# Top-k of the last prompt tile carried in the sample's rounds; probability scales on ScalarE; weight remainders on GpSimd; an order per layer

## Chip, cores and metric

One core of one Trainium2 chip. The metric is the device time of one execution in microseconds. Five engines work side by side: PE (TensorE), DVE (VectorE), ACT (ScalarE), POOL (GpSimd) and SP (SyncE), whose queue issues all data transfers of this kernel.

## What is computed

One inference step of a two-layer encoder trunk on 512 prompt tokens and 64 sample tokens (the sample has 1024 cached keys). Each layer projects the normalised input to the operands of three mixers, merges their gated outputs and projects back:

```python
z = rmsnorm(x, norm_g) @ w_in                     # aq ak av ag | bq bk bv bqi bki bwi bg | cq ck cv cg | mg
# A: differential attention, 4 heads: p = softmax(q k + bias); a = p[0] - lam * p[1]; o = a v
# B: an indexer scores every key; the top k keys of each query stay, the others are masked
score = jnp.einsum('bqh,bqhs->bqs', wi, relu(qi ki)); _, idx = lax.top_k(score, topk)
p = softmax(q k[idx] * 64 ** -0.5 + bias); o = p v[idx]      # topk: 128 for the prompt, 256 for the sample
# C: retention with a decay per head, in chunks
y = x + sum(sigmoid(mg) * (stack([oa * silu(ag), ob * silu(bg), oc * silu(cg)]) @ w_branch)) @ w_out
```

The outputs are y of the prompt and of the sample, the new keys and values, and the states.

## The kernel before

**Tiles.** The 576 tokens are five tiles: four of 128 prompt tokens (t = 0 to 3) and the 64 of the sample (t = 4). A matrix product with a weight is made exact enough from three products of a rounded high part and a remainder: high x high, (input remainder) x high, high x (weight remainder). `wload` fetches 512 x 256 weights into `wraw`, ACT writes the high part `whi` (L495), and DVE the remainder `wlo = wraw - whi` (L496, 128x1024). `wlo` has two buffers and `wraw` two; a projection of 1024 rows takes a pair of each. `proj_ch` (L634) keeps channels on the partitions (288 columns a product), `proj_tok` (L613 to L622) tokens (256 columns). Both issue the `whi` products of an output tile first and the `wlo` products last. PSUM has three tiles for projections (`pj`), two for scores (`s`) and three for transposes and small outputs (`t`).

**Mixer B's top-k.** `idx_prompt` and `idx_sample` leave scores in SBUF: `SC[t]` for t = 1, 2, 3 (128 partitions, 256, 384 and 512 columns) and `SC[4]` for the sample (64 partitions, 1088 columns; the other 64 partitions of that tile are idle). `topk(t)` finds eight maxima a round (`MAX8`, L829) and strikes them out (`MATCH_REPLACE8`, L830): 16 rounds for a prompt tile, 32 for the sample, and then turns the struck places into 0 and the rest into a large positive number (L831), which `b_prompt` and `b_sample` take as a mask. All of it is on DVE.

**Attention.** For a tile, PE writes scores, DVE adds the bias and finds the minimum (L468, L920, L471), ACT writes the exponential with its sum, DVE takes the reciprocal and multiplies the probabilities by it (L1004 in `a_att`, L1188 in `b_prompt`, L1218 in `b_sample`), and PE transposes them. The bias windows come from a table in DRAM, `grep` (12 heads x 128 rows x 352), which `build_windows` fills by one transfer.

**Norms.** `qknorm` squares on ACT, sums on DVE, takes the power on POOL (L455), multiplies on DVE (L648), multiplies by the gain on POOL (L649); PE's transposes (L946) wait for that.

**The order.** The program is a list of steps (`STEPS`): x: norm of a tile; pw, i, iq: the indexer's weights, projection and queries; w: the bias table; cv, cq, ca: mixer C; aq, ak, av, aa: mixer A; bq, bp, bs: mixer B; g: a gate; s: the split of a gated output; m: the merge of a branch (`branch`, the large products L634); top: the top-k. The steps stand in the same order in both layers, each with a bias for layer 0 and one for layer 1. `Order` records every instruction, gives it its place in the program plus its step's bias as its rank, and plays the program through with a cost for each instruction: each engine takes, of the instructions that are ready, the one of lowest rank. The order of issue so found is pinned on every engine, SP included; an engine's queue runs in that order only.

## Time and profile before

| | |
|---|---|
| median of 3 runs | 1444.93 us (1444.91 to 1447.29) |
| the profiled execution | 1446.73 us, of which the span from first to last instruction 1444.9 |
| PE busy | 1385.6 us, 96% of the span, 10422 products |
| weight loads (PEld) | 1328.2 us, 92% |
| DVE, ACT, POOL busy | 1146.3 (79%), 663.8 (46%), 246.9 us (17%) |
| granted clock of PE, mean | 0.999 |
| DMA engines, mean share; moved | 31.6%; 127.51 MB |

The busy time of PE is that of its records, which overlap: a product's record is longer than the distance to the next product's start. So an engine that waits shortly between two products can still read as busy.

### The profile page before, as it was taken

The numbers are of one execution on the slowest core, as the hardware profiler recorded it, in microseconds if no ns is written. First come the engines' busy times: TensorE is split into PE (matmuls) and PEld (weight loads), VectorE is DVE, ScalarE is ACT, GpSimd is POOL, SyncE is SP. The second block draws the span as 40 slices with busy tenths as digits, with TensorE's granted clock in tenths as the row PEclk, the third lists the DMA queues.
The fourth block names the chain that finished last, engine by engine and source line by source line (L and its number), as shares of the span: only waits on it lengthen the run. The fifth ranks groups of instructions, "written<-read, shape, count | busy, mean of one in ns | idle before, by whom it ended". The sixth has DMA issues, their size and how long they took to land.

```text
span 1444.9 us, 27676 instructions
## 1 busy us (share of the span) xinstructions
PE 1385.6 (96%) x10422; PEld 1328.2 (92%) x10422; DVE 1146.3 (79%) x2791; ACT 663.8 (46%) x1631; POOL 246.9 (17%) x294
## 2 busy tenths in 40 slices
PE   5999999999999999999999999999999999999999
PEld 4899989998999989999989998899989998999999
DVE  5799999998776888844487999999997678886433
ACT  5433464445555464433353335543546454644321
POOL 1121432112223020000030333410321120300000
PEclk9999999999999999999999999999999999999999
DMA  7423225222332222324532222232424322121333
GB/s 220 111 73 86 54 72 141 73 76 86 95 94 61 87 59 59 89 67 115 172 103 64 70 74 77 79 100 70 112 65 114 78 68 61 47 73 47 99 122 115
DMA packets 189738, 127.51 MB, mean 88 GB/s; under 512 B 65976, under 2 KB 188388, under 8 KB 189604
## 3 DMA queue, kind: packets, MB, share of 16 engines
q1 hardware_dynamic: 189604, 125.74, 31.1%
q8 instruction: 82, 1.34, 0.4%
q14 instruction: 52, 0.43, 0.1%
HBM read 114.84 MB, written 13.03 MB: 88 GB/s over the span
## 4 chain that ended last, share of the span: by engine, by line
PE 64%; DVE 20%; ACT 6%; DMA 5%; issue 3%; SPq 1%; POOL 1%; DVEq 0%; ACTq 0%
PE pj L634 29%; PE pj L622 11%; PE pj L1352 6%; DVE wlo L496 4%; DVE u L830 3%; DMA wraw<-in_w_in_dram 3%; DVE m L829 3%; PE s L1181 1%; PE t L1193 1%; ACT whi L495 1%; DVE s L468 1%; PE s L998 1%; DVE u L956 1%; PE t L1013 1%; PE t L1045 1%
## 5 line engine op out<-in xcount | busy, mean ns | idle before, releaser
L495 ACT CAST whi<-wraw 128x1024 fp32r<-128x1024 f32 x164 | 172.0, 1049 | 186.6 <-DMA wraw<-in_w_in_dram 73.3
L496 DVE TENSOR_TENSOR wlo<-wraw,whi 128x1024 fp32r<-128x1024 f32 x164 | 199.3, 1226 | 64.7 <-PE pj L634 53.0
L634 PE MATMUL pj<-xh,whi 128*128 128x288 f32 x1216 | 205.9, 299 | 5.3 <-ACT sg L1265 1.9
L634 PE MATMUL pj<-xh,wlo 128*128 128x288 f32 x1216 | 199.8, 297 | 3.9 <-DVE wlo L496 3.9
L634 PE MATMUL pj<-xl,whi 128*128 128x288 f32 x1216 | 200.4, 297 | 0.0
L634 PEld LDWEIGHTS pj<-xh,whi 128*128 128x128 f32 x1216 | 175.0, 188 | 9.1 <-ACT sg L1265 2.3
L634 PEld LDWEIGHTS pj<-xh,wlo 128*128 128x128 f32 x1216 | 173.4, 188 | 7.0 <-DVE wlo L496 5.6
L634 PEld LDWEIGHTS pj<-xl,whi 128*128 128x128 f32 x1216 | 174.1, 188 | 1.2 <-issue 0.3
L829 DVE MAX8 m<-u 64x8 f32<-64x1088 f32 (+3 forms) x160 | 134.9, 845 | 1.7
L830 DVE MATCH_REPLACE8 u<-m,u 64x1088 f32<-64x1088 f32 (+3 forms) x160 | 133.1, 832 | 0.1
L622 PE MATMUL pj<-wlo,xh 128*128 128x256 f32 x768 | 121.5, 289 | 6.5 <-DVE wlo L496 6.4
L455 POOL TENSOR_TENSOR ssn<-ssn,mh 128x4 f32<-128x4 f32 (+1 forms) x70 | 73.2, 1048 | 318.6 <-DVE ssn L454 313.1
L634 PE MATMUL pj<-u,whi 128*128 128x288 f32 x768 | 126.1, 297 | 0.0
L622 PE MATMUL pj<-whi,xh 128*128 128x256 f32 x768 | 117.8, 287 | 3.6 <-ACT whi L495 2.4
L622 PE MATMUL pj<-whi,xl 128*128 128x256 f32 x768 | 115.2, 285 | 0.0
L622 PEld LDWEIGHTS pj<-wlo,xh 128*128 128x128 f32 x768 | 103.1, 191 | 10.0 <-DVE wlo L496 8.5
L634 PEld LDWEIGHTS pj<-u,whi 128*128 128x128 f32 x768 | 110.1, 188 | 0.7
L622 PEld LDWEIGHTS pj<-whi,xh 128*128 128x128 f32 x768 | 102.2, 190 | 6.5 <-ACT whi L495 3.7
L622 PEld LDWEIGHTS pj<-whi,xl 128*128 128x128 f32 x768 | 101.7, 191 | 0.4
L1265 ACT ACTIVATE sg<-pj 128x288 f32<-128x288 f32 x96 | 39.2, 410 | 77.9 <-PE pj L634 77.1
L634 PE MATMUL pj<-u,wlo 128*128 128x288 f32 x384 | 70.5, 299 | 1.2 <-DVE wlo L496 1.2
L1352 PE MATMUL pj<-whi,u 128*128 128x256 f32 x512 | 68.8, 282 | 0.4 <-ACT u L1287 0.4
(280 smaller groups left out, 2547.1 us busy)
## 6 DMA issues: line engine op xcount, KB each, us to landing
wraw<-in_w_in_dram SPq DMA_DIRECT2D x116, 512.0 KB, 3.8
wraw<-in_w_branch_dram SPq DMA_DIRECT2D x24, 512.0 KB, 4.7
wraw<-in_w_out_dram SPq DMA_DIRECT2D x16, 512.0 KB, 4.7
wraw<-in_w_in_dram SPq DMA_DIRECT2D x20, 256.0 KB, 3.4
r<-in_cache_a_k_dram SPq DMA_DIRECT2D x64, 64.0 KB, 2.3
r<-in_cache_a_v_dram SPq DMA_DIRECT2D x16, 256.0 KB, 2.9
out_dram<-u SPq DMA_DIRECT2D x32, 128.0 KB, 2.1
D<-grep SPq DMA_DIRECT2D x24, 112.0 KB, 2.0
```

Of the source, the lines that this page charges most:

```text
L455: ptt(ss, ss, mh[:ss.shape[0], :1].to_broadcast(list(ss.shape)), op=OP.pow)
L468: nc.vector.tensor_tensor_reduce(s, s, d, 1.0, init, OP.add, OP.min, out)
L495: nc.scalar.copy(hi[:, :n], raw[:, :n])
L496: tt(lo[:, :n], raw[:, :n], hi.bitcast(F32)[:, :n], op=OP.subtract)
L622: mm(ps[:M, :ncol], a[:, k, q], b[:, k, :ncol], start=(i == 0 and k == 0), stop=(i == 2 and k == 7))
L634: mm(ps[:, :288], a[:, k, c], b[:, k, q], start=(i == 0 and k == 0), stop=(i == 2 and k == kt - 1))
L829: nc.vector.max(m8[:rows], sc)
L830: nc.vector.match_replace(sc, m8[:rows], sc, SENT)
L956: tt(W_[2 + c][r] if which else w[x], tv[r], w.bitcast(F32)[r], op=OP.subtract)
L998: mm(s[:, :w], Q[c][:, hh, tq], K[c + 2 * i][:, hh, :w], start=i == 0, stop=i == 1)
L1265: lambda q, ps: act(sg[:, q], ps, AF.Tanh, scale=0.5))
L1352: mm(ps[:M, :256], src[:, c0:c0 + M], (hv, hv, lv)[i][:, k], start=(i == 0 and k == 0), stop=(i == 2 and k == 7))
```

## The change

Five things change together.

1. `topk(3)` no longer exists. The upper half of prompt tile 3's scores (partitions 64 to 127) is copied into the idle partitions of the sample's score tile and goes through its first 16 rounds, the lower half through its last 16. The rounds of the sample run on 128 partitions x 1088 columns; the columns past 512 of the carried half are filled with the hidden value.
2. The probabilities are multiplied by their reciprocal on ACT (`Copy` with a scale per partition) in `a_att`, `b_prompt` and `b_sample`; the factor 0.5 goes into the reciprocals first.
3. A step marked `*` (17 in layer 0, 16 in layer 1) makes its weight remainders on POOL, not on DVE; the first remainders of layer 0 are on POOL and those of layer 1 on DVE, the reverse of before.
4. The bias table is built in four parts by steps of their own (`wg0` to `wg3`), each by way of SBUF, and its rows have another pitch.
5. Each layer has its own list of steps. A step has up to four numbers: a bias for all engines, one more for those other than PE and SP, one more for SP, and a spread over the step's instructions. The planner's costs are changed, transfers most.

```diff
-STEPS = """
-pw0+-2700/-3200 x0+0/-3900 x1+-11000/0 x2+3500/1700 x3+3900 w0+300/-5700 x4+-7800/0 i0+9200/4200 iq0+9300/5200
...
+STEPS = ("""
+x0+1500,-14100,-8500 x2+-25200,-11100,400 x1+800,-13500 w0+1800,600,200 x3+25700,1000,-800 x4+12300,-14200,3800
+wg2+-8300,-2400,1500 pw0*+5000,4400,6600 wg1+1000,-3400,1700 i0+-16000,1600,5900 iq0*+-11800,-7900,3600 aq0+-4000
...
         if e == "SP":
-            for o in outs[:1]:
-                n = cols(o) * o.ap[0][1]
-            return n / 90.0
+            n = cols(outs[0]) * outs[0].ap[0][1]
+            run = min(self._run(o) for o in ins[:1] + outs[:1])
+            return n / run * max(36.0, run / 6.0) / 16
...
-                return max(n * 0.4375 + 7, 112.0)
+                return max(n * 0.4375 + 7, 112.0) * 1.02
...
+            late = bias[0] + (0 if e == "PE" else bias[2] if e == "SP" else bias[1])
...
-        dma(grep, bass.AP(tensor=gdram.tensor, offset=gdram.offset, ap=[[352, 12], [0, 128], [1, 352]]))
+
+    def spread_windows(g):
+        rows = sb(1152, "u")[:, :1056]
+        dma(rows, bass.AP(tensor=gdram.tensor, offset=gdram.offset + 1056 * g, ap=[[0, 128], [1, 1056]]))
+        dma(grep[g].rearrange("p h c -> p (h c)"), rows)
...
             nc.scalar.copy(hi[:, :n], raw[:, :n])
-            tt(lo[:, :n], raw[:, :n], hi.bitcast(F32)[:, :n], op=OP.subtract)
+            (ptt if beside[0] else tt)(lo[:, :n], raw[:, :n], hi.bitcast(F32)[:, :n], op=OP.subtract)
...
         def topk(t):
-            sc = SC[t]
-            rows = sc.shape[0]
-            for r in range(32 if t == 4 else 16):
-                m8 = sb(8, "m8")
-                nc.vector.max(m8[:rows], sc)
-                nc.vector.match_replace(sc, m8[:rows], sc, SENT)
-            ts(sc, sc, SENT, -NEG, op0=OP.not_equal, op1=OP.mult)
-            if t == 4:
-                nc.scalar.copy(SC["all"][64:128, :NKS], sc)
+            def rounds(sc, n):
+                for r in range(n):
+                    m8 = sb(8, "m8")
+                    nc.vector.max(m8[:sc.shape[0]], sc)
+                    nc.vector.match_replace(sc, m8[:sc.shape[0]], sc, SENT)
...
+            if t < 3:
+                rounds(SC[t], 16)
+                mask(SC[t], SC[t])
+            elif t == 4:
+                both, prompt = SC["all"][:, :NKS], SC[3]
+                half = both[64:128, :512]
+                nc.vector.memset(both[64:128, 512:], HIDE)
+                nc.scalar.copy(half, prompt[64:128])
+                rounds(both, 16)
+                mask(prompt[64:128], half)
+                nc.scalar.copy(half, prompt[0:64])
+                rounds(both, 16)
+                mask(half, half)
+                nc.scalar.copy(prompt[0:64], half)
+                mask(SC[4], SC[4])
+                nc.scalar.copy(both[64:128], SC[4])
...
-                    ts(P[1][:, :n], P[1][:, :n], Z[:, 1:2], None, op0=OP.mult)
+                    act(P[1][:, :n], P[1][:, :n], AF.Copy, scale=Z[:, 1:2])
...
+                ts(Z, Z, 0.5, None, op0=OP.mult)
                 for h in range(4):
-                    ts(P[h][:, :n], P[h][:, :n], Z[:, h:h + 1], 0.5, op0=OP.mult, op1=OP.mult)
+                    act(P[h][:, :n], P[h][:, :n], AF.Copy, scale=Z[:, h:h + 1])
...
+                ts(z, z, 0.5, None, op0=OP.mult)
                 for p in (P[0], P[1], P[2][:, :192]):
-                    ts(p, p, z, 0.5, op0=OP.mult, op1=OP.mult)
+                    act(p, p, AF.Copy, scale=z)
...
-                ready["w"] = wload_idx(l, tt if l == 0 else ptt)
+                ready["w"] = wload_idx(l, ptt if beside[0] else tt)
...
-        for step in STEPS.split():
+        for step in STEPS[l].split():
             step, _, late = step.partition("+")
-            with order.bias(int(late.split("/")[min(l, late.count("/"))] or 0)):
-                run(step)
+            beside[0] = step.endswith("*")
+            with order.bias(([int(x) for x in late.split(",") if x] + [0, 0, 0, 0])[:4]):
+                run(step.rstrip("*"))
```

The order of issue moves on every engine. Three places follow; line numbers are those of either kernel, and a name's number tells tiles of one kind apart.

SP at the start of layer 0, before: `wraw` are the indexer's weights, `u` the input tiles, `P` here the norm's gain.

```order
L508 DMA wraw_113<-in_w_in_dram 128x4x128
L508 DMA wraw_113<-in_w_in_dram 128x4x68
L508 DMA wraw_122<-in_w_in_dram 128x4x128
L508 DMA wraw_122<-in_w_in_dram 128x4x68
L411 DMA u_63<-in_x_prompt_dram 128x512
L541 DMA u_64<-in_x_prompt_dram 128x1024
L411 DMA u_63<-in_x_prompt_dram 128x512
L413 DMA cs_70<-in_consts_dram 128x192
L1298 DMA cs_70<-in_consts_dram 128x332
L533 DMA P_82<-in_norm_g_dram 128x512
L533 DMA P_83<-in_norm_g_dram 128x512
L572 DMA gqka_86<-in_a_qk_g_dram 128x128
```

The same queue now:

```order
L448 DMA u_63<-in_x_prompt_dram 128x512
L585 DMA u_65<-in_x_prompt_dram 128x1024
L448 DMA u_63<-in_x_prompt_dram 128x512
L450 DMA cs_70<-in_consts_dram 128x192
L577 DMA P_86<-in_norm_g_dram 128x512
L577 DMA P_87<-in_norm_g_dram 128x512
L616 DMA gqka_90<-in_a_qk_g_dram 128x128
L617 DMA gqkb_91<-in_b_qk_g_dram 128x128
L621 DMA gcol_96<-in_a_subln_g_dram 128x1
L622 DMA gcol_96<-in_c_gn_g_dram 128x1
L627 DMA z_101<-in_a_lambda_dram 128x256
L585 DMA u_64<-in_x_prompt_dram 128x1024
```

The first half of tile 0, the second half and the gain (`P`) stood at places 5, 7, 10 and 11 of the queue and now stand at 1, 3, 5 and 6; the four weight transfers went from places 1 to 4 to places past 15.

DVE in layer 0, in mixer C's time, before: rounds of tile 3's top-k (`MAX` with 128 partitions, `MATCH_REPLACE` over 512 columns) between the remainders of the weights (L496) and the outputs of gates.

```order
L829 MAX m_3143<-u_764 128x8
L876 MEMSET sso_1896 128x1
L847 SCALAR_TENSOR_TENSOR u_1181<-u_1181,pj_1236 128x288
L830 MATCH_REPLACE u_764<-m_3143,u_764 128x512
L496 TENSOR_TENSOR wlo_1427<-wraw_1425,whi_1426 128x1024
L829 MAX m_3146<-u_764 128x8
L847 SCALAR_TENSOR_TENSOR u_1181<-u_1181,pj_1263 128x288
L830 MATCH_REPLACE u_764<-m_3146,u_764 128x512
L888 SCALAR_TENSOR_TENSOR u_1181<-t_1414,gcol_92,u_1181 128x512
L891 SCALAR_TENSOR_TENSOR u_1181<-t_1420,gcol_92,u_1181 128x64
L829 MAX m_3149<-u_764 128x8
L496 TENSOR_TENSOR wlo_1433<-wraw_1431,whi_1432 128x1024
```

DVE now, at rounds of the sample with the carried half (1088 columns):

```order
L872 MAX m_3797<-u_2385 128x8
L907 SCALAR_TENSOR_TENSOR u_2274<-u_2274,pj_2329 128x288
L486 MEMSET D_4929 64x64
L873 MATCH_REPLACE u_2385<-m_3797,u_2385 128x1088
L540 TENSOR_TENSOR wlo_2442<-wraw_2440,whi_2441 128x1024
L907 SCALAR_TENSOR_TENSOR u_2274<-u_2274,pj_2356 128x288
L540 TENSOR_TENSOR wlo_2448<-wraw_2446,whi_2447 128x1024
L872 MAX m_3800<-u_2385 128x8
L873 MATCH_REPLACE u_2385<-m_3800,u_2385 128x1088
L689 TENSOR_REDUCE ssn_2480<-pj_2452 128x4
L872 MAX m_3803<-u_2385 128x8
```

The 32 rounds over 512 columns (16 a layer) are nowhere in the queue any more; the sample's 64 rounds have 128 partitions in place of 64.

POOL in layer 0 at mixer A's first projections, before: powers (L455) and gain products (L649) of the norms, and remainders of cached keys (L672).

```order
L455 TENSOR_TENSOR ssn_2441<-ssn_2441,mh_72 128x4
L649 TENSOR_TENSOR z_2438<-z_2438,gqka_86 128x256
L455 TENSOR_TENSOR ssn_2482<-ssn_2482,mh_72 128x4
L649 TENSOR_TENSOR z_2479<-z_2479,gqka_86 128x256
L455 TENSOR_TENSOR ssn_2523<-ssn_2523,mh_72 128x4
L649 TENSOR_TENSOR z_2520<-z_2520,gqka_86 128x256
L455 TENSOR_TENSOR ssn_2564<-ssn_2564,mh_72 128x4
L649 TENSOR_TENSOR z_2561<-z_2561,gqka_86 128x256
L672 TENSOR_TENSOR u_3172<-r_3174,u_3171 128x512
L672 TENSOR_TENSOR u_3172<-r_3185,u_3171 128x512
```

POOL at such a projection now:

```order
L497 TENSOR_TENSOR ssn_2618<-ssn_2618,mh_72 128x4
L716 TENSOR_TENSOR u_3002<-r_3004,u_3001 128x512
L716 TENSOR_TENSOR u_3002<-r_3015,u_3001 128x512
L693 TENSOR_TENSOR z_2615<-z_2615,gqka_90 128x256
L497 TENSOR_TENSOR ssn_2659<-ssn_2659,mh_72 128x4
L540 TENSOR_TENSOR wlo_2817<-wraw_2815,whi_2816 128x1024
L693 TENSOR_TENSOR z_2656<-z_2656,gqka_90 128x256
L540 TENSOR_TENSOR wlo_2823<-wraw_2821,whi_2822 128x1024
L716 TENSOR_TENSOR u_3432<-r_3434,u_3431 128x512
L540 TENSOR_TENSOR wlo_2935<-wraw_2933,whi_2934 128x1024
L716 TENSOR_TENSOR u_3432<-r_3445,u_3431 128x512
```

Remainders of weights (L540, 128x1024) stand between a power and the gain product of the same projection, and between the remainders of cached keys. Over the whole queue 74 such rows are new, and 74 of 164 are gone from DVE's.

## Rows read from the trace of the kernel before

**Rows 1.** Stretches of the span; columns: length, then busy time of each engine (its instructions), granted clock.

```profile
0.00:36.00 36.00, 20.19 (x114) 16.99 (x114) 21.33 (x69) 19.30 (x52) 5.23 (x17) 1.00 0.76 221
36.00:325.00 289.00, 279.28 (x2141) 267.49 (x2142) 276.50 (x664) 126.08 (x317) 68.92 (x86) 1.00 0.32 86
325.00:722.00 397.00, 387.26 (x2909) 373.84 (x2909) 278.76 (x680) 193.10 (x471) 49.88 (x50) 1.00 0.32 90
...
759.00:1084.00 325.00, 313.02 (x2402) 299.68 (x2401) 304.63 (x700) 145.62 (x352) 79.30 (x93) 1.00 0.29 80
1084.00:1408.00 324.00, 316.89 (x2336) 303.60 (x2336) 224.31 (x568) 154.99 (x371) 32.09 (x31) 1.00 0.27 78
...
sum 1444.90, PE 1385.60 PEld 1328.24 DVE 1146.27 ACT 663.83 POOL 246.89; mean PE 197.94 PEld 189.75 DVE 163.75 ACT 94.83 POOL 35.27
```

**Rows 2.** The chain that ended last, one long piece: start, length, what.

```profile
621.71 52.34 PE pj L634 x392
```

**Rows 3.** Groups by line, engine PE: the 288-column product.

```profile
L634 PE MATMUL pj<-xh,whi 128*128 128x288 f32 x1216 | 205.9, 299 | 5.3 <-ACT sg L1265 1.9 <-DVE u L847 1.8 <-DVE sg L1274 1.1
```

**Rows 4.** Waits of engine PE: total, times, longest (us).

```profile
PE s L562 <- DVE u L557: 12.5, 1, 12.5
PE pj L622 <- DVE wlo L496: 6.4, 7, 1.7
PE pj L634 <- DVE wlo L496: 5.1, 7, 1.2
PE t L946 <- POOL z L649: 3.9, 4, 2.2
PE s L1181 <- ACT P L1184: 3.8, 10, 0.9
```

**Rows 5.** Groups by line and shape, engine DVE: x, then busy us and mean ns of one.

```profile
L496 DVE TENSOR_TENSOR wlo<-wraw,whi 128x1024 fp32r<-128x1024 f32 x164 | 199.3, 1226 | 64.7 <-PE pj L634 53.0 <-PE pj L1352 6.0 <-PE pj L1345 3.1
L829 DVE MAX8 m<-u 64x8 f32<-64x1088 f32 x64 | 81.9, 1280 | 0.3
...
L829 DVE MAX8 m<-u 128x8 f32<-128x512 f32 x32 | 22.0, 687 | 0.4
L830 DVE MATCH_REPLACE8 u<-m,u 128x512 f32<-128x512 f32 x32 | 21.5, 673 | 0.0
...
L1188 DVE TENSOR_SCALAR P<-P,Z 128x512 f32<-128x512 f32 x16 | 6.6, 475 | 0.0
...
L1188 DVE TENSOR_SCALAR P<-P,Z 128x128 f32<-128x128 f32 x16 | 4.2, 311 | 0.1
...
L465 DVE TENSOR_TENSOR qd<-qks,qd 64x64 fp32r<-64x64 f32 x16 | 3.5, 218 | 0.7 <-ACT qd L464 0.5
```

**Rows 6.** Groups by line and shape, engine ACT.

```profile
L878 ACT ACTIVATE P<-o 128x512 f32<-128x512 f32 x16 | 10.0, 641 | 0.3
...
L1000 ACT ACTIVATE P<-s,nm 128x128 f32<-128x128 f32 x16 | 5.9, 368 | 3.2 <-DVE nm L468 1.5 <-DVE sso L880 1.2 <-PE t L1045 0.4
```

**Rows 7.** Groups by line and shape, engine POOL.

```profile
L649 POOL TENSOR_TENSOR z<-z,gqka 128x256 f32<-128x256 f32 x40 | 34.0, 851 | 60.6 <-DVE ssn L454 18.4 <-DVE z L648 15.1 <-PE s L998 5.7
L672 POOL TENSOR_TENSOR u<-r,u 128x512 fp32r<-128x512 f32 x24 | 33.2, 1393 | 94.2 <-ACT u L671 81.2 <-PE t L1041 12.6 <-POOL sso L455 0.3
```

**Rows 8.** Timeline of the first 40 us, all engines.

```profile
3.89 0.43 SPq L411 DMA_DIRECT2D u<-in_x_prompt_dram  x1
...
5.64 0.90 SPq L533 DMA_DIRECT2D P<-in_norm_g_dram  x2
...
11.73 2.74 DVE L557 SCALAR_TENSOR_TENSOR u<-u,ss,P 128x512 f32<-128x512 f32 x4 [0.50 <-POOL ss L455]
```

**Rows 9.** Timeline of 226.5 to 232 us, engine POOL: start us, us, what.

```profile
226.96 2.46 POOL L649 TENSOR_TENSOR z<-z,gqka 128x256 f32<-128x256 f32 x1 [1.58 <-DVE z L648]
```

**Rows 10.** The same stretch of the timeline, engine DVE.

```profile
226.72 1.21 DVE L496 TENSOR_TENSOR wlo<-wraw,whi 128x1024 fp32r<-128x1024 f32 x1
...
230.51 1.30 DVE L465 TENSOR_TENSOR u<-qks,u 128x64 fp32r<-128x64 f32 x1
```

More of the change, by code (lines that the diff above doesn't have):

```diff
@@ L168, in _area, with _run @@
         return t.name, p0, p0 + o.ap[0][1], m << off
+    @staticmethod
+    def _run(o):
+        n = 1
+        for s, k in reversed(list(o.ap)):
+            if k > 1 and s != n:
+                break
+            n *= k
+        return n
     def _cost(self, i, e, ins, outs):
@@ L196, in _cost @@
         ptr = op in ("TensorScalarPtr", "ISA") and len(ins) > len(wide) and n > 4
-        return 68 + n * (0.52 if fast else 1.042) + 61 * ptr
+        return 70 + n * (0.53 if fast else 1.065) + 62 * ptr + moved
     def _shared(self, e, op, ins, outs):
@@ L224, in _graph @@
             acc = [(self._area(o), False) for o in ins] + [(self._area(o), True) for o in outs]
+            acc = [x for x in acc if x[0][0][:3] not in ("in_", "out")]
             for (t, p0, p1, m), w in acc:
@@ L242, in _graph @@
             begun -= done | {k}
-            ops.append((i, e, done, begun, self._cost(i, e, ins, outs), k + bias, self._shared(e, str(i.opcode), ins, outs)))
+            late = bias[0] + (0 if e == "PE" else bias[2] if e == "SP" else bias[1])
+            where.append((step, size[step], bias[3]))
+            size[step] += 1
+            ops.append((i, e, done, begun, self._cost(i, e, ins, outs), k + late, self._shared(e, str(i.opcode), ins, outs)))
+        for k, (step, at, spread) in enumerate(where):
+            o = ops[k]
+            ops[k] = o[:5] + (o[5] + int(spread * at / size[step]),) + o[6:]
         return ops, users
@@ L420, in trunk @@
         nc.gpsimd.memset(p[:, 192:], 0.0)
-    grep = dram.tile([12, 128, 352], F32, name="grep")
+    gdram = dram.tile([12, 352], F32, name="gdram")
+    grep = [dram.tile([128, 3, 352], F32, name=f"grep{g}") for g in range(4)]
     yscr = dram.tile([NTOK, DM], F32, name="yscr")
@@ L479, in __getitem__ @@
             return self.parts[ix[1] // 4][(ix[0], ix[1] % 4) + tuple(ix[2:])]
+    beside = [False]
     def wload(srcs, kt):
```

77 lines of the change are left out of this document (50 added, 27 removed).

## The prediction

> **What bounds the kernel.** I read the stretches first [rows 1]. PE is busy for 1385.60 of 1444.90 us, and its products are the same 10422 after the change, so only its 59.3 us of idle time and what its records hide can be won. The idle time by stretch, length less busy time: 15.8 us up to 36 us, 9.7 from 36 to 325, 9.7 from 325 to 722, 12.0 from 759 to 1084, 7.1 from 1084 to 1408, and 5.0 in what is left (the change of layer and the tail). DVE's share is 96% from 36 to 325 (276.50 of 289) and 94% from 759 to 1084, but 70% and 69% in the two other long stretches. Where DVE is full, PE idles 3.4% and 3.7%; where it is not, 2.5% and 2.2%. So DVE is second to PE, in two stretches of 614 us in all.
>
> Undisturbed, PE runs 392 products of 288 columns in 52.34 us, 133.5 ns apart [rows 2]. The record of one lasts 299 ns [rows 3]. A wait of up to some 165 ns therefore leaves no idle time, and a longer one shows that much too short. The weight loads, with shorter records, idle 116.7 us by the sum in [rows 1], 46.8 of them in the two full stretches and 43.5 in the two others. I take the true waits to lie between the two counts.
>
> The waits say who is late [rows 4]: the first product of all waits 12.5 us; then the weight remainder `wlo` from DVE (6.4 and 5.1 us, 7 times each, at most 1.7), the norm's gain product from POOL (3.9 in 4) and the probabilities from ACT (3.8 in 10). The rest is scattered. No single wait is worth a per cent.
>
> **The change, part by part.**
>
> *Top-k of tile 3.* 32 rounds go, each 0.687 + 0.673 us [rows 5]: 43.5 us less on DVE. The sample's rounds get 128 partitions for 64. A `MAX8` over 1088 columns on 64 partitions takes 1280 ns, 1.18 ns a column, and one over 512 columns on 128 partitions 687 ns, 1.34 ns a column [rows 5]: by columns there is no surcharge for more partitions to be seen, and I charge nothing. One more mask and a fill a layer come to about 1 us each layer, priced like a 512-column scale (0.475 us) [rows 5]. The order puts the sample's last round well before mixer B's scores of tile 3, with over 100 us of PE's products between, so that the later mask makes nobody wait.
>
> *Scales.* 120 multiplications leave DVE: 24 of 128 columns, 32 of 192 or 256, 32 of 384 and 32 of 512. In `b_prompt` the smallest takes 0.311 us and the largest 0.475 [rows 5]; at the middle, 0.393 us, that is 47 us. ACT gets them at 0.368 to 0.641 us [rows 6], the nearest rows of 128 and 512 columns, in the middle 0.50 us: 61 us, which takes it from 46% to 50% of the span. Each scale ends about 0.1 us later than on DVE, in front of PE's transposes. The merges' large products stand ready beside them, so I charge 1 us; uncovered it would be at most 120 x 0.17 = 20 us. 24 short multiplications of the sums come to DVE, about 4 us at 0.16 us, half a 128-column scale.
>
> *Remainders on POOL.* 74 of the 164 `wlo` leave DVE: 74 x 1.226 = 90.7 us [rows 5]. POOL has no such row. Its two-input products take 851 ns at 256 columns and 1393 at 512 [rows 7]; the line through both gives 2.48 us at 1024 columns. The ends are 1.4 us (no shorter than 512 columns) and 2.8 (twice 512); I take 2.5, since the line passes through two rows. That is 185 us more on POOL, 432 in all, 30% of the span.
>
> DVE's sum: 1146 - 43.5 - 47 + 6 - 90.7 = 971 us, 67%. In the two full stretches all 43.5 us of the rounds, some 40 of the moved remainders (49 us, by the order) and about 10 us of scales fall away: 581 us of work become about 479, 78% of 614, near the share of the other stretches.
>
> What that is worth to PE. The lower end is that the full stretches come down to the 2.3% of the others: 614 x (3.5% - 2.3%) = 7.4 us. The upper end is all of their idle time, 21.7 us. I take the middle, 14.5. In the other two stretches the change is one of order: two lists and three biases in place of one. Nothing there has a price in a row; the ends are all 16.8 us of idle time won, and half as much lost. I take 6 won, a third, because DVE's remainders are released earlier there too. What the records hide [rows 3] I add as a quarter of both, 5 us, well under the 1:2 of the two counts. Together 25.5 us.
>
> *What POOL's remainders cost.* A remainder can begin only when PE has left the buffer, and PE must have other products meanwhile. In the order, 22 of the 74 have less than 2.9 us of PE's products (at 120 to 133.5 ns each) between the last use of the buffer and the first of the new content; most of these have about 2.8. With 2.5 us for the work and some tenths for the two hand-overs, they are late by about 0.2 us: 22 x 0.2 = 4.4 us. The ends are nothing, and 22 x 1.6 = 35 us, if each meets the hold-up of the next part.
>
> *The start.* The first product waits for the normalised tile 0, whose gain `P` is issued at 5.64 us and whose second half at 3.89, behind four weight transfers [rows 8]; DVE begins at 11.73. Ahead of the queue they are issued some 2 to 3 us sooner. The weights come later, but three tiles of transposes stand before the first product with them. I take 2.5 us won, between 0 and 4. The bias table's four parts stand behind what the start needs; nothing is charged.
>
> Sum: -25.5 + 4.4 + 1 - 2.5 = -22.6 us. The profiled execution took 1446.73 us, 1.8 above the median of 1444.93. So 1424.1 on its scale and **1422.3 us** as a median.
>
> One rule speaks for more. The Trainium skill (Perfetto Trace Analysis, Identifying the Most-Contended Engine) says that busy matmul time is a poor measure of how near TensorE is to its limit, and that the weight loads' busy share is the better one. By it the waits to be won are the larger count, and the same shares of it would give about 40 us; no row here separates the two.
>
> **The rivals.**
>
> *A: nearly all waits go.* For: DVE loses 15% of its load, and the waits [rows 4] are each short. Against: the waits for ACT stay and get more work. Start 4, 21.7 of the full stretches, 12 of the others, 10 hidden, nothing lost to POOL: -47, **1398 us**.
>
> *B: the waits only move.* For: the stretches where DVE has 30% to spare still idle 2.2 to 2.5% [rows 1], so most of these are matters of order, not of load. Then -7.4 - 2.5 + 8 (half as much again lost in the others): about -2, **1443 us**, not to be told from no change.
>
> *C: POOL's queue becomes the late one, slower.* POOL and DVE hold each other up. At 226.96 us a gain product of 256 columns took 2.46 us, 851 ns on the mean [rows 7, 9], where DVE was in a `wlo` [rows 10]; and right behind, at 230.51, DVE's remainder of 64 columns took 1.30 us, where such work takes 218 ns [rows 5, 10]. Each moved remainder is a block of 2.5 us of this kind, and in the order it stands between a power and a gain product of the same norm, for which PE's transposes wait. PE waits there already, with POOL at 17% [rows 1, 4]. If half of the 74 reach PE with 1.2 us (half a block), that is 44 us lost against 27 won: +17, **1462 us**. It decides from where a moved remainder costs PE 27 / 74 = 0.36 us on the mean. The Trainium skill (SBUF — State Buffer, Who interferes with whom) has the pair as an exclusive lock held for a whole instruction, the loser blocked, against DVE work with two SBUF inputs; the rows at 226.96 and 230.51 us agree with that. Against C: the rounds of the top-k have one input and the scores' work reads PSUM, and much of DVE's queue in these stretches is of these kinds, so that a block lies beside work that goes on; and the order gives most remainders 2.8 us or more.
>
> That the change does not do what it says can be left out for the top-k: the rounds are gone from the queue.
>
> **How the numbers follow.** About 0.2% (2.9 us) is what a measurement of this kernel can tell from no change. Forecast, between 1408 and 1441 us: 0.65. A: 0.10. B: 0.11. C: 0.14. Of the forecast's case a little ends within 1442, and of B a third falls under it: faster by over 0.2% (under 1442.0) 0.79, within 0.08, slower 0.13. The range leaves out the lower half of A and nearly all of C: 1401 to 1446.
>
> **What would show it.** DVE near 970 us of busy time with no 512-column rounds, and under 85% in the mid-part of both layers; POOL near 430; the moved remainder near 2.5 us; the first product near 10 us; PE's busy time unchanged and its idle time near 35 us. C shows as waits of PE for POOL's `wlo` and `z` above 20 us. The prediction is wrong if PE's idle time stays above 55 us, whoever is named for it.

## The result and the profile after

| | before | changed |
|---|---|---|
| median | 1445.06 us (1444.91 to 1447.29, 4 runs) | 1427.84 us (1426.15 to 1430.57, 4 runs) |
| ratio, 95% interval | | 0.9879 [0.9861, 0.9897] |
| profiled execution; its span | 1446.73; 1444.9 us | 1430.57; 1428.8 us |
| mean granted clock | 0.999 | 0.995 |

The change is 17 us faster, 1.2%. Busy times of the changed kernel (first section of its page):

```profile
PE 1385.6 (97%) x10422; PEld 1330.3 (93%) x10422; DVE 1045.4 (73%) x2529; ACT 721.5 (50%) x1757; POOL 413.1 (29%) x368
```

PE is busy for the same time to 0.01 us; the span fell by 16.1 us, all of it recorded idle time of PE (59.3 to 43.2 us). By stretch, columns as in [rows 1]:

```profile
0.00:36.00 36.00, 24.29 (x128) 20.60 (x129) 23.66 (x80) 20.75 (x58) 12.99 (x24) 1.00 0.75 226
36.00:325.00 289.00, 282.53 (x2178) 271.67 (x2178) 251.44 (x592) 139.13 (x341) 117.16 (x108) 1.00 0.33 91
325.00:722.00 397.00, 388.38 (x2920) 374.36 (x2919) 256.16 (x631) 212.51 (x518) 79.49 (x65) 1.00 0.33 93
722.00:759.00 37.00, 35.46 (x238) 33.94 (x237) 25.66 (x79) 18.74 (x58) 14.53 (x17) 0.90 0.28 79
759.00:1084.00 325.00, 319.05 (x2472) 307.95 (x2472) 273.42 (x627) 158.22 (x380) 139.68 (x120) 1.00 0.31 85
1084.00:1408.00 324.00, 318.25 (x2348) 304.30 (x2348) 209.07 (x515) 170.75 (x404) 49.28 (x38) 0.99 0.28 80
```

PE's idle time went from 15.8 to 11.7 us up to 36 us, from 9.7 to 6.5 up to 325, from 9.7 to 8.6 up to 722, from 12.0 to 5.9 from 759 to 1084 and from 7.1 to 5.8 up to 1408: 9.3 of the 16.1 us came from the two stretches that DVE had filled. DVE's share there is now 87% and 84%.

Idle time is not the whole of it, since records hide short waits. Counted by products (the x of PE), the change is 134 products ahead at 1408 us, and 107 of them it gains in these two stretches (2178 for 2141 and 2472 for 2402). That share of 16.1 us is some 13 us, an estimate, as products differ in length. At the change of layer it falls back by 10; the row of before there is

```profile
722.00:759.00 37.00, 35.20 (x248) 33.09 (x247) 29.62 (x93) 20.86 (x65) 11.47 (x19) 0.95 0.38 101
```

PE's waits in the changed kernel, against [rows 4]:

```profile
PE s L606 <- DVE u L601: 9.3, 1, 9.3
PE t L1068 <- DVE P L1065: 4.3, 4, 1.9
PE s L606 <- ACT s L1427: 3.6, 2, 2.2
PE t L1006 <- POOL z L693: 1.5, 2, 1.1
...
PE pj L678 <- POOL wlo L540: 0.2, 1, 0.2
```

The 11.5 us for `wlo` from DVE are gone (0.3 us is left). The wait for ACT at the change of layer has grown from 1.6 to 3.6 us, and that for mixer A's probabilities `P` from DVE from 0.2 to 4.3; before they were

```profile
PE s L562 <- ACT s L1361: 1.6, 1, 1.6
...
PE t L1008 <- DVE P L1005: 0.2, 1, 0.2
```

The costliest rows of DVE and POOL by shape, against [rows 5, 7]:

```profile
L540 DVE TENSOR_TENSOR wlo<-wraw,whi 128x1024 fp32r<-128x1024 f32 x90 | 115.1, 1287 | 65.1 <-PE pj L678 47.8 <-PE pj L1418 5.9 <-ACT whi L539 4.3
L872 DVE MAX8 m<-u 128x8 f32<-128x1088 f32 x64 | 82.3, 1287 | 1.0 <-ACT u L888 0.7
...
L1338 DVE TENSOR_TENSOR acc<-acc,sg 128x288 f32<-128x288 f32 x32 | 19.9, 633 | 0.4
...
L1063 DVE TENSOR_TENSOR Z<-Z,nlam 128x1 f32<-128x1 f32 x32 | 12.7, 397 | 0.2
```

```profile
L540 POOL TENSOR_TENSOR wlo<-wraw,whi 128x1024 fp32r<-128x1024 f32 x74 | 179.5, 2440 | 415.9 <-PE pj L678 203.9 <-ACT whi L539 130.2 <-PE pj L659 31.4
```

A round's `MAX8` takes the same on 128 partitions as on 64 (1287 and 1280 ns), so the carried half costs the rounds nothing. A remainder on POOL takes 2440 ns, but small two-input work on DVE has become longer than before:

```profile
L1276 DVE TENSOR_TENSOR acc<-acc,sg 128x288 f32<-128x288 f32 x32 | 14.3, 451 | 0.2
...
L1003 DVE TENSOR_TENSOR Z<-Z,nlam 128x1 f32<-128x1 f32 x32 | 4.7, 146 | 0.1
```

### The profile page after: what moved, and what is told of

The parts are those of the page before. It is cut to its first block, busy times and chain, and to the rows that moved or that the text cites. A ratio compares the mean times of both kernels' runs of the same rounds, so it can differ in the third digit from the quotient of the medians.

```text
span 1428.8 us, 27701 instructions
## 1 busy us (share of the span) xinstructions
PE 1385.6 (97%) x10422; PEld 1330.3 (93%) x10422; DVE 1045.4 (73%) x2529; ACT 721.5 (50%) x1757; POOL 413.1 (29%) x368
## 5 line engine op out<-in xcount | busy, mean ns | idle before, releaser
L540 POOL TENSOR_TENSOR wlo<-wraw,whi 128x1024 fp32r<-128x1024 f32 x74 | 179.5, 2440 | 415.9 <-PE pj L678 203.9
L678 PE MATMUL pj<-xh,wlo 128*128 128x288 f32 x1216 | 205.3, 299 | 0.1
L540 DVE TENSOR_TENSOR wlo<-wraw,whi 128x1024 fp32r<-128x1024 f32 x90 | 115.1, 1287 | 65.1 <-PE pj L678 47.8
L497 POOL TENSOR_TENSOR ssn<-ssn,mh 128x4 f32<-128x4 f32 (+1 forms) x70 | 67.0, 961 | 176.2 <-DVE ssn L496 173.9
L666 PE MATMUL pj<-wlo,xh 128*128 128x256 f32 x768 | 115.2, 285 | 0.3 <-DVE wlo L540 0.3
L872 DVE MAX8 m<-u 128x8 f32<-128x1088 f32 (+2 forms) x128 | 113.6, 887 | 2.0 <-ACT u L888 0.7
L873 DVE MATCH_REPLACE8 u<-m,u 128x1088 f32<-128x1088 f32 (+2 forms) x128 | 112.0, 875 | 0.1
```

Source lines behind the costliest of these rows:

```text
L497: ptt(ss, ss, mh[:ss.shape[0], :1].to_broadcast(list(ss.shape)), op=OP.pow)
L540: (ptt if beside[0] else tt)(lo[:, :n], raw[:, :n], hi.bitcast(F32)[:, :n], op=OP.subtract)
L666: mm(ps[:M, :ncol], a[:, k, q], b[:, k, :ncol], start=(i == 0 and k == 0), stop=(i == 2 and k == 7))
L678: mm(ps[:, :288], a[:, k, c], b[:, k, q], start=(i == 0 and k == 0), stop=(i == 2 and k == kt - 1))
L872: nc.vector.max(m8[:sc.shape[0]], sc)
L873: nc.vector.match_replace(sc, m8[:sc.shape[0]], sc, SENT)
```

## Experiments

Each ran beside runs of before on the same chip, whose median was 1447.7 to 1448.8 us; the changed kernel itself did not run there, and its ratio of 0.9879, taken over, is about 1430.5 us. Differences below are differences of ratios, at 1448 us. A ratio's interval is 0.1 to 0.35% wide to either side, so a difference to the change is known to some 3 to 6 us.

| run | median, us | ratio to before, interval | to the change |
|---|---|---|---|
| a_order_only | 1471.59 | 1.0162 [1.0146, 1.0177] | +41 |
| b_ops_all | 1514.77 | 1.0457 [1.0439, 1.0474] | +84 |
| b_start | 1446.21 | 0.9985 [0.9975, 0.9995] | +15 |
| a_square_sbuf | 1424.63 | 0.9834 [0.9817, 0.9851] | -6.5 |
| k_pool | 1445.05 | 0.9975 [0.9961, 0.9989] | +13.9 |
| k_scale | 1438.29 | 0.9928 [0.9909, 0.9948] | +7.1 |
| q_pool | 1505.45 | 1.0389 [1.0354, 1.0424] | +74 |
| a_no_carry | 1450.54 | 1.0006 [0.9990, 1.0022] | +18 |
| k_load | 1474.42 | 1.0184 [1.0159, 1.0209] | +44 |
| k_all | 1501.11 | 1.0363 [1.0346, 1.0379] | +70 |
| a_old_costs | 1476.59 | 1.0188 [1.0167, 1.0209] | +45 |
| k_relief | 1426.77 | 0.9847 [0.9820, 0.9874] | -5 |

### The order alone, the operations alone

**a_order_only**: the change's lists, biases, planner costs and table steps, with the operations of before.

```diff
-                rounds(both, 16)
+                rounds(SC[3], 16)
+                mask(SC[3], SC[3])
+                rounds(SC[4], 32)
...
-            beside[0] = step.endswith("*")
+            beside[0] = False
...
-                    act(P[h][:, :n], P[h][:, :n], AF.Copy, scale=Z[:, h:h + 1])
+                    ts(P[h][:, :n], P[h][:, :n], Z[:, h:h + 1], 0.5, op0=OP.mult, op1=OP.mult)
```

> The changed kernel with its two lists, biases, planner costs and bias-table steps, but with the operations of before: tile 3's 16 rounds of its own (just ahead of the sample's 32, inside the same step), probabilities scaled on DVE, all weight remainders on DVE. Theory 'load' (the 17 us came from the work taken off DVE, the lists only fit it): DVE is back near 1146 us of busy time, PE's idle time back at 55 to 60 us, 1440 to 1448 us. Theory 'order' (the lists alone brought it): 1427 to 1433 us. Half and half: 1434 to 1439.

**b_ops_all**: the reverse, the list and costs of before with all three changed operations.

```diff
-            for r in range(32 if t == 4 else 16):
+                rounds(both, 16)
...
-            tt(lo[:, :n], raw[:, :n], hi.bitcast(F32)[:, :n], op=OP.subtract)
+            (ptt if beside[0] else tt)(lo[:, :n], raw[:, :n], hi.bitcast(F32)[:, :n], op=OP.subtract)
...
-                    ts(P[h][:, :n], P[h][:, :n], Z[:, h:h + 1], 0.5, op0=OP.mult, op1=OP.mult)
+                    act(P[h][:, :n], P[h][:, :n], AF.Copy, scale=Z[:, h:h + 1])
```

> The kernel before with its own list and planner costs, but with the operations of the change: carried top-k, scales on ACT, remainders on POOL in the same steps as in the change. Theory 'load': most of the gain without any new list, 1430 to 1436 us. Theory 'order': nothing without the lists, 1443 to 1452 us, since POOL's remainders fall where the list has no room for them. DVE near 1045 us of busy time, POOL near 413, in either case.

Every time was missed, by both theories; DVE's and POOL's busy times in b_ops_all came as expected (1048.1 and 412.8 us). The order alone is 24 us slower than before (1.0162), the operations alone 66 us slower (1.0457), both together 17 us faster. In the first, PE waits for DVE's remainders:

```profile
PE pj L678 <- DVE wlo L540: 13.8, 10, 3.3
...
PE pj L666 <- DVE wlo L540: 7.9, 8, 2.4
```

In the second, for nearly everything at once, the remainders on POOL among it:

```profile
PE pj L637 <- DVE u L866: 8.8, 3, 6.3
PE pj L637 <- POOL wlo L499: 7.7, 4, 2.9
PE s L1200 <- ACT P L1203: 5.9, 11, 1.8
```

Part of both losses is slower products and not idle time: PE is busy for 1400.7 and 1412.8 us, at mean granted clocks of 0.988 and 0.981. Both kernels are planned anew, so load and plan move together. The next runs hold one of them still.

### One load at a time, with the queues held

In the runs named k_ and q_ the planner is told the engine and the price that an instruction had in the kernel it comes from; only then is the instruction put on another engine, at the place of its planned start. All other instructions of all five queues stay in their order. Instructions added in k_load are not shown to the planner.

```diff
-            e = str(i.engine).split(".")[-1]
+            e, price = self.planned.get(i.name, (str(i.engine).split(".")[-1], None))
...
-            order[e].append(k)
+            order[str(ops[k][0].engine)].append(k)
```

**k_pool**: the change with its 74 moved remainders back on DVE.

```diff
-            (ptt if beside[0] else tt)(lo[:, :n], raw[:, :n], hi.bitcast(F32)[:, :n], op=OP.subtract)
+            with order.as_if("Pool" if beside[0] else "DVE"):
+                tt(lo[:, :n], raw[:, :n], hi.bitcast(F32)[:, :n], op=OP.subtract)
```

> The changed kernel with every queue kept exactly as the planner wrote it for the change (all five engines in the same order), and only the 74 moved remainders back on DVE, each at the place in DVE's queue where POOL would have begun it. DVE gets 74 x 1.29 = 95 us back, POOL loses 181 us, the port of the two is free of 74 long blocks. Theory 'load' (what the change won, it won by taking work off DVE; its 17 us go with the some 180 us taken off, so 95 us of them are worth about 9): about 1.006 to 1.009 times the changed kernel, on this chip 1438 to 1442 us; DVE over 78% of the span and PE waiting for DVE's remainders again. Theory 'fit' (what counts is that queues and operations agree; each remainder now takes 1.29 us where the plan left 2.44): the same or a little faster than the changed kernel, 1424 to 1432 us, PE's idle time 40 to 45 us. Above 1450 us would be a third case: DVE's queue holds up what stands behind the inserted remainder.

13.9 us slower, somewhat more than "load" gave, and without its signs: DVE is at 75% of the span, for over 78% expected, and PE waits 2.8 us for DVE's remainders. Where it is lost:

```profile
36.00:325.00 289.00, 278.06 (x2123) 267.05 (x2122) 254.64 (x604) 137.42 (x337) 67.56 (x84) 0.99 0.33 90
325.00:722.00 397.00, 388.33 (x2917) 375.19 (x2917) 259.05 (x634) 211.00 (x509) 45.87 (x49) 1.00 0.33 91
...
759.00:1084.00 325.00, 310.65 (x2398) 298.35 (x2397) 282.48 (x626) 151.06 (x359) 70.03 (x87) 1.00 0.30 82
```

PE is busy 4.5 and 8.4 us less in the two full stretches than in the change, and as busy between 325 and 722. So what the remainders on POOL are worth on these queues, they are worth in the full stretches. And DVE's busy time rose to 1077.2 us, by 32, though 74 x 1226 ns = 90.7 us came back. Not all of the 59 us between is hold-up, since DVE's records overlap too: added up, they come to 1169.9 us in the change and 1209.8 us here, 40 us more. The other 51 us are what POOL's blocks had cost DVE; with the same queues and without them the stretched work is short again:

```profile
L1347 DVE TENSOR_TENSOR acc<-acc,sg 128x288 f32<-128x288 f32 x32 | 14.1, 450 | 0.4
...
L1072 DVE TENSOR_TENSOR Z<-Z,nlam 128x1 f32<-128x1 f32 x32 | 7.3, 229 | 0.2
```

**k_scale**: the change with the 120 scales back on DVE, its queues held.

```diff
-                    act(P[h][:, :n], P[h][:, :n], AF.Copy, scale=Z[:, h:h + 1])
+                    with order.as_if("Activation"):
+                        ts(P[h][:, :n], P[h][:, :n], Z[:, h:h + 1], None, op0=OP.mult)
```

> The changed kernel with every queue kept as it is, and only the 120 scales of probabilities back on DVE, each at the place in DVE's queue where ACT would have begun it. DVE gets 120 x 0.39 = 47 us back, ACT loses 67 us. Theory 'load': 47 of some 180 us are worth 4 to 5 us, about 1434 to 1436 us on this chip. Theory 'fit': a scale on DVE is shorter by 0.1 to 0.2 us, but stands behind whatever DVE is at (a round of 1.28 us, a remainder of 1.29 us), which the plan did not foresee: PE's transposes of the probabilities wait for P from DVE, 120 places at a few tenths of a us, 1440 to 1460 us.

7.1 us slower, between the two theories. DVE rises by 41 us to 1086.4. Little of it is lost in the full stretches (PE busy 0.3 and 2.0 us less), most in the others: from 1084 to 1400 us PE is busy 306.53 us, for 310.25 in the change. PE now waits 7.6 us for `P` from DVE in mixer A (4.3 in the change).

**q_pool**: the reverse of k_pool: the queues of before held, the remainders of the same 33 steps on POOL.

```diff
-            tt(lo[:, :n], raw[:, :n], hi.bitcast(F32)[:, :n], op=OP.subtract)
+            with order.as_if("DVE"):
+                (ptt if beside[0] else tt)(lo[:, :n], raw[:, :n], hi.bitcast(F32)[:, :n], op=OP.subtract)
```

> The kernel before with every queue kept exactly as it was planned for DVE, and only the remainders of the same 33 steps put on POOL, each at the place in POOL's queue where DVE would have begun it: 74 of them leave DVE (91 us), and POOL gets 181 us. No re-planning, so nothing but the load and the later end of each remainder changes. Theory 'load': DVE falls to some 1055 us and the two stretches where it was full gain half of what the change gained, 1436 to 1441 us. Theory 'fit': each moved remainder ends 1.2 us later or more, and 2.44 us of exclusive port stand against DVE's small products where the plan had none; the queue of PE has its products where the remainder was due on DVE, so PE waits for wlo from POOL over 30 us in all: 1470 to 1520 us, most of the 67 us that all three operations cost on the queue of before.

```profile
PE pj L646 <- POOL wlo L508: 17.2, 18, 2.1
PE pj L634 <- POOL wlo L508: 16.2, 18, 2.5
```

Slower than before by 56 us, 0.76 us for each moved remainder; "fit" holds. How much of it is the remainder's later end and how much the hold-up by its block, this run does not separate. DVE lost only 22 us of busy time (to 1124.2). The same 74 instructions win 14 us on the queues planned for them and lose 56 us on those that were not.

**a_no_carry**: the change planned anew with tile 3's own rounds (the first lines of the diff of a_order_only).

> The changed kernel, planned anew, with tile 3's 16 rounds by themselves again just ahead of the sample's 32 rounds on 64 partitions; the scales stay on ACT and the remainders on POOL. DVE gets 32 x 1.36 = 43.5 us back and nothing else moves to another engine. Theory 'load': 43.5 of some 180 us are worth 4 to 5 us, 1434 to 1437 us on this chip. Theory 'fit': the lists and biases were fitted to rounds that take half as long, and the plan that comes out for 64 more instructions is another one in each stretch: slower by more than the load accounts for, 1440 to 1460 us, with holes of PE and a granted clock under 0.95 in slices where neither kernel had them.

18 us slower, as "fit" had it; this mixes 43.5 us of load with another plan. So as much load was put on the queues of the change, held. **k_load**:

```diff
                     nc.vector.max(m8[:sc.shape[0]], sc)
+                    if r * twice // n < (r + 1) * twice // n:
+                        nc.vector.max(m8[:sc.shape[0]], sc)
...
-                rounds(both, 16)
+                rounds(both, 16, 8)
...
-                rounds(both, 16)
+                rounds(both, 16, 9)
```

> The changed kernel with every queue kept as it is, and 34 more MAX8 on DVE: 17 of the sample's 32 rounds a layer issue their MAX8 twice, each second one right behind the first (same data, same result). That is 34 x 1.28 = 43.7 us of DVE work, as much as the 32 rounds of tile 3 that the change took away (43.5 us), without a new plan, without another port holder (one input) and without another wait. Theory 'load, by the price of the remainders' (95 us back on DVE cost 14 us with the queues kept): 43.7 x 0.15 = 6 to 7 us, about 1437 us on this chip, lost in 144 to 325 us and 864 to 1084 us where the rounds stand. Theory 'deadline' (the rounds are one chain that ends just before the sample's softmax, so each us there counts in full or not at all): under 1433 us if the chain has room, 1450 us and more with PE waiting for the sample's mask or for what stands behind the rounds on DVE if it has none. The same edit under a new plan cost 18 us (1450.5).

44 us slower for 34 x 1.295 = 44.0 us of work: each us counts in full. "Load, by the price of the remainders" fell; "deadline" gave the size, but its reason is only half right: PE waits for what stands behind the rounds on DVE and POOL (10.2 us for `P` from DVE, 9.5 for `z` from POOL), hardly for a mask. It is not the change undone, for the place is another: before, tile 3's rounds ran from 93 to 137 us and from 809 to 854 us; k_load puts its work among the sample's, from 184 to 353 us and from 915 to 1080 us. What the carrying by itself is worth, no run shows.

**k_relief** goes the other way:

```diff
-                    nc.vector.max(m8[:sc.shape[0]], sc)
-                    nc.vector.match_replace(sc, m8[:sc.shape[0]], sc, SENT)
+                    c = sc[:, :8] if r * short // n < (r + 1) * short // n else sc
+                    nc.vector.max(m8[:sc.shape[0]], c)
+                    nc.vector.match_replace(c, m8[:sc.shape[0]], c, SENT)
```

> The opposite of k_load. The changed kernel with every queue kept, and 18 of the sample's 64 rounds (4 and 5 of each 16) done over 8 columns in place of 1088: the instructions stay, at their places, but DVE has about 18 x (2.56 - 0.15) = 43 us less to do in 180 to 324 and 900 to 1008 us, where it is 97 and 99% busy in the changed kernel and where k_load lost 1 us for each us added. The sample's mask and tile 3's are not the reference's, since those rounds find nothing beyond 8 columns. Theory 'corner' (in these stretches DVE and PE are both at their limit, so work added counts in full, and work taken away is worth no more than what PE idles there, 3.7 and 2.6 us, with as much again in what stands behind): 4 to 12 us faster than the changed kernel, 1418 to 1426 us on this chip, DVE falling to some 85% there. Theory 'DVE bounds' (each us off the rounds is a us won, in both directions): 1390 us. Theory 'order' (PE's idle time there is set by single waits, not by DVE's fill): within 3 us of the changed kernel, 1427 to 1433 us.

About 5 us faster; the interval just overlaps the change's, so between nothing and 9 us, for 34 us less of DVE's busy time (1011.5). "DVE bounds" is out. 1426.8 us lies between the ranges of "corner" and "order", and the time alone does not tell them apart. The two stretches in which the rounds stand, before, in the change, in k_load and in k_relief:

```profile
180.00:324.00 144.00, 138.22 (x1057) 134.06 (x1056) 142.49 (x297) 69.39 (x177) 30.21 (x30) 1.00 0.34 91
900.00:1008.00 108.00, 103.98 (x785) 100.64 (x786) 106.20 (x234) 54.54 (x139) 20.09 (x19) 1.00 0.31 85
```

```profile
180.00:324.00 144.00, 140.26 (x1069) 135.53 (x1068) 139.52 (x291) 79.22 (x193) 44.01 (x37) 1.00 0.36 99
900.00:1008.00 108.00, 105.37 (x817) 101.74 (x816) 106.73 (x232) 58.79 (x151) 41.67 (x29) 1.00 0.36 96
```

```profile
180.00:324.00 144.00, 126.94 (x952) 121.21 (x950) 140.29 (x279) 70.59 (x175) 32.38 (x28) 0.99 0.31 83
900.00:1008.00 108.00, 95.74 (x722) 91.25 (x721) 105.96 (x216) 56.14 (x141) 35.95 (x27) 1.00 0.30 83
```

```profile
180.00:324.00 144.00, 140.10 (x1072) 135.72 (x1070) 123.14 (x292) 79.15 (x193) 45.07 (x37) 1.00 0.36 97
900.00:1008.00 108.00, 105.07 (x817) 101.72 (x816) 96.76 (x234) 59.47 (x153) 41.21 (x30) 1.00 0.36 97
```

DVE (third busy time) is full in all but the last: 97 and 99% in the change too, while PE is at 97 and 98%. Both are nearly full together. Work added to DVE makes PE late (140.26 to 126.94 us busy in the first stretch, 44 us in the whole kernel); work taken away leaves PE where it is (140.10 and 105.07 us, 1072 and 817 products for 1069 and 817) and shows as idle time of DVE. PE's 6.4 us of idle time there do not fall, which speaks for "order": single waits set them, not DVE's fill.

**k_all**: k_pool, k_scale and k_load together.

> The changed kernel with every queue kept and all three loads back on DVE at once: the 74 remainders, the 120 scales and the 34 doubled MAX8. It has the operations' load of the kernel before on the queues of the change. Theory 'loads add up': 14 (remainders) + 7 (scales) + what k_load shows (some 7), about 1458 us on this chip. Theory 'room': the change left DVE spare time that one load at a time may use, and all three together use up more than there is, so the sum is larger than its parts: 1465 to 1480 us, near the 1471.6 of the same operations under a new plan. Theory 'plan': most of the loss of the new plan (1471.6) came from the planning, and with the queues kept it is gone: under 1450 us.

70 us, the parts' sum being 65: within the intervals they add up. The 1458 us of that theory were missed because k_load's part is 44 us, not 7. Planned anew, nearly the same load costs 41 (a_order_only), so the planner wins back 29 us of it; on before's own list it runs 24 us faster still.

**a_old_costs**: the change with the planner's costs of before; the chip does the same work in another order.

```diff
-            return n / run * max(36.0, run / 6.0) / 16
+            return n / 90.0
...
-                return max(n * 0.4375 + 7, 112.0) * 1.02
+                return max(n * 0.4375 + 7, 112.0)
...
-                clock[e] = t + 500
+                clock[e] = t + 475
```

> The changed kernel with the planner's old prices for the instructions and DMA issues (the lists, the biases and the operations stay those of the change), so the queues are another plan of the same list. Nothing that the chip computes differs, only the order. Theory 'fit' (biases were fitted to one plan; any other plan of the same list is worse): 1440 to 1465 us, that is 10 us or more lost with DVE and POOL as busy as in the change. Theory 'load' (the lighter DVE gives the gain whatever the plan is in detail): within 5 us of the changed kernel, 1428 to 1435 us.

45 us slower with DVE at 1055.1 and POOL at 409.6 us, so with the load of the change. "Fit" holds and was still too small.

### Two single places

**b_start**: before, with the step of the indexer's weights (`pw0`) behind the norms of tiles 0 and 1 and its bias for layer 0 at 0; the list serves both layers.

```diff
-pw0+-2700/-3200 x0+0/-3900 x1+-11000/0 x2+3500/1700
+x0+0/-3900 x1+-11000/0 pw0+0/-3200 x2+3500/1700
```

> The kernel before, with the step of the indexer's weights moved behind the norms of tiles 0 and 1 in the list, so that SP issues tile 0 and the gain first, as the change does. If the start is worth what the first product gained (12.5 to 9.3 us): 1441.5 to 1443 us. If the weights that now come later take it back: 1445 us, with the first product at 9 to 10 us all the same.

About 2 us faster, between the two cases. The longest wait at the start falls from 12.5 to 9.0 us, but two others grow (2.6 us, on another input, and 1.7 us before):

```profile
PE t L690 <- DVE ssn L454: 3.7, 1, 3.7
...
PE t L431 <- DMA rb<-in_rel_bias_dram: 2.8, 1, 2.8
```

The change shows the same: its first product comes at 9.29 us (12.54 before), and its first product with a weight at 17.24 us (17.39 before).

**a_square_sbuf**: at the change of layer, ACT writes the squares that it sums over `xr` in SBUF, no longer into a PSUM tile of the two for scores.

```diff
-                    jk = pb("s")
-                    act(jk[:M, :256], y, AF.Square, accum_out=PSQ[t][:M, u:u + 1])
+                    act(xr[:M], y, AF.Square, accum_out=PSQ[t][:M, u:u + 1])
```

> The changed kernel, where at the end of layer 0 the squares of the new rows are written over the residual tile in SBUF and no longer into one of the two PSUM score tiles that the next layer's transposes need. In the changed kernel PE idles 1.4 and 2.2 us at 717 to 721 us for those squares and the granted clock of 714 to 750 us is 0.86. Theory 'slots' (the transposes wait for their turn of the PSUM tile, behind the squares of all tiles): both waits go and the clock stays at 1.00, 1419 to 1423 us. Rival 'norm chain' (they wait for the norm itself): no difference, 1427 to 1429 us.

6.5 us faster than the change, the lowest ratio of all kernels run; "slots" had it still faster, at 1419 to 1423 us with a clock of 1.00. PE's timeline there (start, length, what), in the change and then in this run:

```profile
717.76 0.66 PE L606 MATMUL s<-cs,u 128*128 128x128 f32 x4 [1.43 <-ACT s L1427]
720.62 1.12 PE L606 MATMUL s<-cs,u 128*128 128x128 f32 x4 [2.21 <-ACT s L1427]
721.39 1.00 PE L792 MATMUL pj<-whi,xh 128*128 128x392 f32 x2
722.19 0.85 PE L792 MATMUL pj<-wlo,xh 128*128 128x392 f32 x2
722.85 0.85 PE L792 MATMUL pj<-whi,xh 128*128 128x392 f32 x2
```

```profile
715.36 1.03 PE L606 MATMUL s<-cs,u 128*128 128x128 f32 x8
...
719.45 0.52 PE L792 MATMUL pj<-whi,xh 128*128 128x392 f32 x2
719.81 0.52 PE L792 MATMUL pj<-wlo,xh 128*128 128x392 f32 x2
```

The transposes into `s` had waited 3.6 us for ACT's squares, and after the two waits a pair of 392-column products took 0.66 to 0.80 us where it takes 0.36 undisturbed. The granted clock from 714 to 750 us is 0.86 in the change, 0.95 in this run. PE does 223 products in those 36 us, for 196. By finer stretches the change has the lower of the clock's two levels (0.50, 1.2 GHz) twice, around the second of these waits and behind it, and again behind a wait of 1.0 us for DVE that ends at 735.8 us:

```profile
719.00:726.00 7.00, 5.38 (x22) 5.38 (x23) 6.21 (x15) 1.68 (x4) 1.06 (x2) 0.51 0.70 208
...
736.00:740.00 4.00, 4.00 (x18) 3.53 (x17) 2.63 (x7) 1.95 (x5) 0.82 (x2) 0.57 0.10 19
```

This run has the second alone:

```profile
730.00:734.00 4.00, 3.89 (x16) 3.70 (x17) 2.30 (x5) 1.53 (x4) 0.00 (x0) 0.57 0.06 12
```

So "slots" holds for the two waits, and the clock falls once more for another reason. This run was planned anew too, so not all of the 6.5 us need be from this place.

## Why the prediction was right, point by point

The forecast's case came: faster by 17.2 us, for 22.6 forecast, with PE's idle time at 43.2 us for 35. The place and the direction were right; most terms were off, and that the sum came near is in part luck.

**DVE's sum was mis-sized: 1045 us for 971.** Two things make up most of the 74 us. The step took 90.7 us off for the remainders and counted nothing for what their longer stay on POOL does to DVE's other work, though it had both rows of the hold-up [rows 9, 10] and used them for rival C alone, as a price of PE's. k_pool measures it: 51 us, over half of what was taken off. And it took lengths of records off a busy time in which records overlap: all of DVE's records come to 1294.9 us before, in 1146.3 us of busy time, and to 1169.9 us in 1045.4 after. The overlap fell by 24 us, and by so much a sum of lengths is too large. The Trainium skill (SBUF — State Buffer, Who interferes with whom) has a DVE instruction with two SBUF inputs blocked for a whole GpSimd instruction that reads SBUF, when that one came first; the trace agrees, as the addition to `acc` has a mean of 633 ns with the remainders on POOL, the longest 2403 ns, and 450 without, in the same queue.

**The full stretches.** Forecast: DVE at 78%, 14.5 us of idle time won and a quarter of that, 3.6 us, in hidden waits. DVE came to 85% (524.9 of 614 us), and 9.3 us of idle time went, some 13 us by products. The place was right, and k_pool shows it: what it loses, it loses there. But the picture of a DVE with 22% to spare was wrong. Where the rounds stand it stays 97 to 99% full, and yet 44 of the 107 products are gained there (1069 for 1057 and 817 for 785). The price of DVE's work has two values there: k_load pays 1 us for each us added, k_relief gets between nothing and 0.3 for each us taken off. The step spread one price over 614 us.

**Top-k.** Nothing for the 64 further partitions was right (82.3 us for 64 `MAX8`, 81.9 before). What the 43.5 us taken off are worth was not measured at their place; k_load shows only that as much work would cost 44 us among the sample's rounds.

**The order** was put at 6 us, between half as much lost and all won. The ends were far too narrow: another plan of the same work is 45 us slower (a_old_costs), the list without its operations 24 us slower than before. What the order is worth by itself can't be told, since it is worth something only with its operations; another list for the operations of before was not tried. In the two stretches (to 722, and 1084 to 1408) 2.5 us of idle time went.

**Remainders late on POOL**: 4.4 us forecast; PE's waits show 0.2 us of it. 2440 ns for 2.5 us was right. Rival C's signs are absent: PE waits 2.2 us in all for POOL's `wlo` and `z`, where C had over 20. Some hold-up does reach PE, by way of DVE: its wait for `P` in mixer A, 4.3 us for 0.2 before, is 1.6 us in k_pool. On the queues of before the loss is real: q_pool pays 0.76 us for each remainder, against the 0.36 from which C was to win, and its waits name `wlo`. So what keeps C off is that the queues were planned for the remainders on POOL. One of C's rows was misread: the 218 ns beside the 1.30 us are a 64x64 product's; the 128x64 product has a mean of 529 ns before, blocks included, and 280 in k_pool.

**Hidden waits**: 5 us forecast. PE's busy time did not fall, but in the full stretches some 4 us went (13 by products, 9.3 of idle time), and as much came elsewhere; the lower granted clock (0.995 for 0.999, the change of layer above all) is part of that, the rest is open. The weight loads idle 98.5 us, for 116.7: 18 us less, much as the products' 16. The larger count held no larger gain, so the 40 us that the prediction had worked out by the Trainium skill's rule (Perfetto Trace Analysis, Identifying the Most-Contended Engine) did not come.

**Scales and start.** The scales cost 67 us of ACT (the sum of their records) for the 61 forecast, and k_scale shows what their move is worth on these queues, 7 us; the 1 us charged for later probabilities is not to be seen: the wait for `P` in mixer A gets longer still, 7.6 us, with the scales back on DVE. The start was right in size (2.5 forecast, b_start about 2, 14 products or some 2 us in the change). The bias table's four parts have no run of their own.

**Not foreseen**: the longer wait at the change of layer, 3.6 us for 1.6, with a granted clock of 0.86 over the 36 us around it, where before had 0.95 (722 to 759 us); a_square_sbuf wins some 6 us, its new plan included.

So the sum came near with most of its parts too large. For the stretches it has 25.5 us less 5.4 us of charges (POOL, later probabilities), 20.1 net; some 16 came by products, 12 by idle time. The ground given for the largest part, a DVE with room to spare, did not come, and so far that part is near by luck.

## What to carry to other kernels

Where two engines are both nearly full, load can have a kink: here 44 us added to the second cost 44 us, and 34 us taken off it won 9 us at most. Read the share in the sub-stretch where the movable work stands, not over the whole stage. Work moved to POOL is not all gone from DVE when both read SBUF: count what its blocks hold up, here over half of what was moved. Before lengths of records are taken off a busy time, compare their sum with it. And in a kernel with pinned queues an operation on an order that was not planned for it says little (here 56 us lost, and 14 us won on the queues planned for it): hold the queues and move one operation to see its price there.

## What the runs showed of the hardware

- Beside POOL's blocks of 2440 ns even a 128x1 product of two inputs gets longer on DVE: 146 ns on the mean before, 397 in the change, 229 with the remainders back on DVE.
- A `MAX8` over 1088 columns takes 1287 ns on 128 partitions and 1280 on 64.
- Around two waits of PE of 1.43 and 2.21 us the granted clock fell to 0.50 (1.2 GHz): PE ran some 5 us of products at it, and a pair of 392 columns took 0.66 to 0.80 us for 0.36. Half of 5 us is 2.5 us, an estimate of the loss, on top of 3.6 us of waits; a_square_sbuf, without both, is 6.5 us faster. Before, behind one wait of 1.61 us, the clock fell too (0.66 from 731 to 736 us).
